# A hybrid transformer block: weight sums, spills, reloads and output DMAs moved between queues and in order

## The chip, the cores and the metric

One core of a Trainium2 chip runs the whole kernel. Its engines are PE (TensorE, matrix products), DVE (VectorE), ACT (ScalarE), POOL (GpSimd) and SP (SyncE, which here only issues DMAs). Each engine works through its own instructions in order. The metric is the device time of one execution in microseconds (us); the kernel before has a median of 2313.04 us in 3 runs (2312.16 to 2316.35).

## The reference

512 latent tokens and 256 context tokens of width 1024 go through two layers with shared weights. In short:

```
for l in range(2):
    sh1, sc1, g1, sh2, sc2, g2 = split(silu(c) @ w_ada[l] + b_ada[l])      # 6 modulation vectors, latents
    (the same for the context tokens, from c_ctx)
    h = rms_norm(x) * norm1_g * (1 + sc1) + sh1
    glu, q, k, v, rq, rk, rv, rg, gates = split(h @ w_in[l] + b_in[l])
    a   = silu(layer_norm(dwconv31(glu_a * sigmoid(glu_b))))                # convolution branch
    att = softmax attention: 8 query heads, 2 key/value heads, rotary, context keys for all
    ret = retention in both directions, chunks of 128, decay per head, group norm * silu(rg)
    y   = (ga * (a @ w_pa) + gb * (att @ w_pb) + gc * (ret @ w_pc)) @ w_out[l]
    x   = x + g1 * y
    h   = rms_norm(x) * norm2_g * (1 + sc2) + sh2
    gt, val = split(h @ w_up[l])                                            # 2 x 2816 columns
    x   = x + g2 * ((silu(dwconv3(gt)) * val) @ w_down[l])
out = rms_norm(x) * final_norm_g                                            # latents only
```

The context tokens do the same with their own modulation; in the last layer they only give keys, values and retention states.

## The kernel before

Activations lie feature by feature on 128 partitions, tokens along the free axis: a tile `x` is 128 features x 768 tokens. Every product in fp32 is made of three PE products of rounded halves: `whi*hh`, `whi*hl` and `wlo*hh`, where `whi`/`wlo` are the rounded weight and its rest, `hh`/`hl` those of the activation.

**Weights.** SP loads raw tiles of 512 KB (`raw`, `issue`), ACT rounds each to `whi` (L218), DVE subtracts to `wlo` (L219). SP looks two tiles ahead (RAWB).

**Start.** `start` loads x and the columns of `w_ada` in the pieces of START; `first_products` writes out the order of the first norm, of the modulation pieces (`go(stage, column)`) and of the first two column groups of `w_in` by hand, under `in_order`.

**Mixers.** `layer_mixers` goes through the units of ORDER: K, Q keys and queries, R retention inputs, A and C convolution, G gates, P the projection of the branches and T the third gate. Attention, retention, convolution and modulation are generators beside them (`Side`): each PE unit feeds them credit (`tick`), scaled by ATTR, RETR, CONVR and ADAR, and they emit their instructions in between. A scheduler then fixes the order on each engine. Four attention outputs `att` of 128 x 768 are spilled to DRAM (`attsp`, L1497) and reloaded as `rl` (L1503) for `w_pb`; all such tiles share 45 slots, so a new tile may wait until an older one's last reader, a spill too, is done. `ij` (L1583) is a table for retention; `ret_tables` makes `kdec` (L916) and `dec` (L930) from it.

**Sums.** In layer 0 the up-projection of the FFN is done with seven products of blocks in place of eight. Four of them need sums of weight blocks, S1 to S4. `make_sums` has POOL make them in DRAM: a copying DMA (L627) and adding DMAs (L632), six batches of up to four chunks, one batch at each of six units (SUMAT). The first DMA of a batch waits for the PE product before it in program order; S2 needs S1, S4 needs S2.

**Up-projection.** `up_order` lists the products: "11" and "12" for the first UPFIRST chunks, which need only one half of the tokens, then S2, S1, S3 for them, then the rest chunk by chunk. `last_chunks` runs `w_out` before it and steps the norm of the finished half of tokens; `split_tokens` makes the operands `hh`/`hl` (L716, L717) of the blocks.

**Modulation rows.** `ada_rows` makes late modulation vectors on DVE: POOL loads a row tile `rowa` into a raw slot (L588), DVE multiplies by `crow` and adds up (L599). During the down-projection `down` feeds it with ADAR[3]. The last down-projection's `evac` (L1814) adds to x.

**Output.** The final norm multiplies each x tile by `rstd` (L1550) and SP writes it (L1551), 16 DMAs.

Of the kernel before, what the change touches and what calls it, by code (L numbers as in the profile page):

```python
# [18 lines left out]
F32 = mybir.dt.float32  # L19
F32R = mybir.dt.float32r  # L20
AF = mybir.ActivationFunctionType
ALU = mybir.AluOpType
# [16 lines left out]
NSUB = 140  # L39
START = ((0, 256, 2), (256, 256, 0), (512, 256, 4), (768, 256, 0))  # L40
ND = 4
# [7 lines left out]
ATT_LEAD, RET_LEAD = (3, 2), (1, 1)  # L49
ATTR, RETR, CONVR, ADAR = (1.0, 1.0), (1.4, 1.6), (0.4, 0.4), (0.06, 0.28, 0.4, 0.33)  # L50
SUMAT = ("R1", "G1", "G2", "G3", "P1", "P2")
QLAG = 2
# [6 lines left out]
PEP, DVP, LATE = (4,), (2, 3), (5,)  # L59
NADA = 24 + 8 * len(PEP)  # L60
ROWS = 1552
# [35 lines left out]

UPFIRST = 3
CUTS = ((0, 4), (4, 8), (8, 12), (12, 16), (16, NFF))
# [185 lines left out]
class Kern:  # L285
# [92 lines left out]

    def last_chunks(self, key, xs, segs, hold, evac, norm, lead=0, limit=None):
# [14 lines left out]
        ws, tiles = [], []  # L394
        for m in range(KC - hold, KC):
            ws.append([])
            for k in range(n):
                ws[-1].append(self.W.next(key(m, k), P))
                if k == 0:
                    tiles.append(self.W.cur)  # L400
        tiles.append(self.W.cur + (self.W.off == SUB))
        gen = None
        halves = parts(segs)[::-1] if limit else parts(segs)
        for i, hs in enumerate(halves):
            for j, m in enumerate(range(KC - hold, KC)):
# [12 lines left out]
        self.W.release()  # L418
        return gen
# [200 lines left out]

    def make_sums(self, b):

        n = len(batches()[b]) * Q
        src = {x: self.io[f"wup{4 * b + i}"] for i, x in enumerate(BLOCKS)}
        for name, base, more in SUMS:
            t = src[name] = self.up_sums[b][name] = self.dram.tile([P, n], F32, name=f"sum{name}_{b}")
            first = self.nc.gpsimd.dma_start(t, src[base], max_dma_last_dim=2048)  # L627

            info = mybir.DependencyInfo(mybir.DependencyClass.Sync, mybir.DependencyReason.DATA)
            self.tc.add_manual_dep(first.ins, self.last_mm.ins.name, info, reason="later")  # L630
            for x in more:
                self.nc.gpsimd.dma_start(t, src[x], accum_op=ALU.add, max_dma_last_dim=2048)  # L632


    def rstd2(self, pts, name, y=None):
# [501 lines left out]
    def first_products(self, xs, ada):  # L1137
# [9 lines left out]

        def products(k, units=(0, 1)):
            for u in units:
                wh, wl = wb[u][k % 4]  # L1150
                for t in range(n):
                    pt = banks[u][t // 2][:, 256 * (t % 2):256 * (t % 2) + 256]
# [3 lines left out]

        def weights(c):
            self.W.limit = 2 * c + 2
            return [[self.W.next(("w_in", 0, k * P, col), 256) for k in range(4 * c, 4 * c + 4)] for col in (1536, 1024)]

# [5 lines left out]

        for k in range(KC):
            self.sq_add(k, xs[k], ALL, k == KC - 1)
        r = self.S("rstd")
        self.sq_rstd(ALL, r)  # L1170
        go(0, 0)
        go(1, 0)
        go(2, 0)
        banks = [[self.dps() if ND > 3 * u + v else self.ps() for v in range(n // 2)] for u in range(2)]
        t0 = m1(0)
        wb = weights(0)
        m2(t0, 0)
        t1 = m1(1)
        go(0, 256)
        go(1, 256)  # L1180
        m2(t1, 1)
        products(0)
        go(2, 256)
        t2 = m1(2)
        products(1)
        t3 = m1(3)
# [9 lines left out]
        m2(t4, 4)  # L1196
        wb = weights(1)
        go(0, 768)
# [340 lines left out]
    def out_norm(self, xs):  # L1539
# [4 lines left out]
        def gen(segs):  # L1544
# [4 lines left out]
            for k in range(KC):  # L1549
                nc.vector.tensor_tensor(xs[k][:, s], xs[k][:, s], r[:, s], op=ALU.mult)  # L1550
                nc.sync.dma_start(self.io["out"][k][:, s], xs[k][:, s])  # L1551
                yield
        return gen

    def layer_mixers(self, l, last, segs, T, xs, xsp, first, h2):
# [16 lines left out]
        def mixers():  # L1572
# [20 lines left out]
        ths, merged = [], [None] * KC  # L1593
        for step in ORDER[l].split():
            kind, i = step[0], int(step[1:] or 0)
# [49 lines left out]
        def evac(m, pts):  # L1645
            for pt, o, c in kinds(pts):
# [6 lines left out]
        return self.last_chunks(lambda m, k: ("w_out", l, k * P, m * P), mm, even(segs), HOLDO[l], evac, norm, LEADO,  # L1653
                                None if l else NUP + UPFIRST)

    def ffn(self, l, h2, xs, segs, T, gen, xsp, xup):
# [57 lines left out]
        def up_seven():  # L1714
# [37 lines left out]
            def s1(c):  # L1752
                Z[c] = (self.ps() if 0 < c < UPFIRST else self.dps())[:, :HALF]
                product(Z[c], "S1", c)
# [29 lines left out]
            for n, x in enumerate(up_order()):  # L1784
# [8 lines left out]
                elif x[0] != "S2" or x[1] >= UPFIRST:  # L1793
                    steps[x[0]](x[1])
                if n == 0:
                    next(gen)
# [194 lines left out]
```

## Time and profile before

| | us |
|---|---|
| median of 3 runs | 2313.04 |
| profiled execution, its own time | 2318.38 |
| its span | 2316.6 |
| PE busy | 2232.2 (96%) |
| DVE busy | 1604.8 (69%) |
| ACT busy | 989.0 (43%) |
| POOL busy | 144.5 (6%) |

The profile is of one execution. Busy is the time in which an engine works; issuing a DMA counts little. PE and DVE work most, at a mean granted clock of PE of 0.988 of full speed. PE's idle time is the difference between its busy time and the span; where it lies is shown in the rows below. Times there are from the start of the span. In a row `x2` is the number of instructions that it groups, and the square brackets give how long the engine stood idle before it and what released it.

### The profile page before, as it was taken

The numbers are of one execution on the slowest core, as the hardware profiler recorded it, in microseconds if no ns is written. First come the engines' busy times: TensorE is split into PE (matmuls) and PEld (weight loads), VectorE is DVE, ScalarE is ACT, GpSimd is POOL, SyncE is SP. The second block draws the span as 40 slices with busy tenths as digits, with TensorE's granted clock in tenths as the row PEclk, the third lists the DMA queues.
The fourth block names the chain that finished last, engine by engine and source line by source line (L and its number), as shares of the span: only waits on it lengthen the run. The fifth ranks groups of instructions, "written<-read, shape, count | busy, mean of one in ns | idle before, by whom it ended". The sixth has DMA issues, their size and how long they took to land.

```text
span 2316.6 us, 34409 instructions
## 1 busy us (share of the span) xinstructions
PE 2232.2 (96%) x13386; PEld 2037.1 (88%) x13386; DVE 1604.8 (69%) x3219; ACT 989.0 (43%) x1707; POOL 144.5 (6%) x225
## 2 busy tenths in 40 slices
PE   6999968999999989999999989999999999999998
PEld 5988958999999989999999979888887889888887
DVE  6876936889985567565655669878699756744445
ACT  3465643342242346554454434565343434423233
POOL 0001111100010000101101100000001100000000
PEclk9999989999999999999999999999999999999999
DMA  8226894813343333737647521111126623432221
GB/s 304 101 99 173 232 243 126 216 64 117 129 156 128 106 103 100 182 119 191 153 152 183 184 109 56 58 55 58 55 80 222 252 84 111 159 113 97 100 91 37
DMA packets 104466, 307.03 MB, mean 133 GB/s; under 512 B 11024, under 2 KB 13344, under 8 KB 104304
## 3 DMA queue, kind: packets, MB, share of 16 engines
q1 hardware_dynamic: 66240, 186.34, 23.5%
q0 software_dynamic: 38064, 118.50, 18.9%
q8 instruction: 105, 1.72, 0.3%
q14 instruction: 57, 0.47, 0.1%
HBM read 282.26 MB, written 68.68 MB: 151 GB/s over the span
## 4 chain that ended last, share of the span: by engine, by line
PE 53%; issue 3%; DVE 3%; DMA 1%; ACT 1%; POOL 0%; DVEq 0%; POOLq 0%; ACTq 0%
PE pd L319 31%; PE pd L1724 11%; PE ps L319 8%; PE ps L1724 2%; PE ps L1378 1%; DVE wlo L219 1%; DMA crow<-crow 0%; DMA rowa<-wadt 0%; ACT whi L218 0%; DVE cacc L827 0%; DMA rl<-attsp 0%; DVE qq L1326 0%; ACT dx L1805 0%; DMA raw<-wstream 0%; DVE rowa L599 0%
## 5 line engine op out<-in xcount | busy, mean ns | idle before, releaser
L218 ACT ACTIVATE whi<-raw 128x1024 fp32r<-128x1024 f32 x313 | 331.4, 1061 | 748.0 <-PE pd L319 492.0
L219 DVE TENSOR_TENSOR wlo<-raw,whi 128x1024 fp32r<-128x1024 f32 x313 | 382.3, 1222 | 258.8 <-ACT whi L218 245.1
L319 PE MATMUL pd<-hh,whi 128*128 128x384 f32 (+2 forms) x1472 | 471.1, 360 | 0.0
L319 PE MATMUL pd<-hh,wlo 128*128 128x384 f32 (+2 forms) x1472 | 470.2, 359 | 0.0
L319 PE MATMUL pd<-hl,whi 128*128 128x384 f32 (+2 forms) x1472 | 469.5, 359 | 0.0
L319 PEld LDWEIGHTS pd<-hh,whi 128*128 128x128 f32 x1472 | 270.9, 188 | 28.0 <-issue 1.8
L319 PEld LDWEIGHTS pd<-hh,wlo 128*128 128x128 f32 x1472 | 271.4, 188 | 25.9 <-issue 1.1
L319 PEld LDWEIGHTS pd<-hl,whi 128*128 128x128 f32 x1472 | 271.2, 188 | 25.9 <-issue 0.7
L827 DVE SCALAR_TENSOR_TENSOR cacc<-u,vec,cacc 128x497 f32<-128x497 f32 (+9 forms) x360 | 220.9, 650 | 2.0
L1724 PE MATMUL pd<-hh,whi 128*128 128x384 f32 x512 | 171.8, 339 | 9.1 <-ACT hh L716 9.1
L1724 PE MATMUL pd<-hl,whi 128*128 128x384 f32 x512 | 172.3, 336 | 0.5 <-DVE hl L717 0.4
L1724 PE MATMUL pd<-hh,wlo 128*128 128x384 f32 x512 | 171.7, 336 | 0.0
L1361 ACT ACTIVATE prob<-ps,amx,qrs 128x256 f32<-128x256 f32 (+1 forms) x144 | 93.8, 656 | 91.3 <-DVE amx L1356 74.9
L319 PE MATMUL pd<-whi,hl 128*128 128x256 f32 x416 | 120.3, 290 | 5.9 <-DVE hl L784 5.9
L319 PE MATMUL pd<-whi,hh 128*128 128x256 f32 x416 | 120.3, 292 | 2.1 <-ACT hh L781 2.1
L319 PE MATMUL pd<-wlo,hh 128*128 128x256 f32 x416 | 119.3, 287 | 0.0
L319 PE MATMUL pd<-hidh,whi 128*128 128x512 f32 (+1 forms) x302 | 104.1, 356 | 4.0 <-DVE x L1814 4.0
L1724 PEld LDWEIGHTS pd<-hh,whi 128*128 128x128 f32 x512 | 96.5, 189 | 12.0 <-ACT hh L716 10.1
L319 PE MATMUL pd<-hidl,whi 128*128 128x512 f32 (+1 forms) x302 | 103.1, 353 | 0.0
L319 PE MATMUL pd<-hidh,wlo 128*128 128x512 f32 (+1 forms) x302 | 102.9, 354 | 0.0
L599 DVE SCALAR_TENSOR_TENSOR rowa<-rowa,crow 128x768 f32<-128x768 f32 (+1 forms) x144 | 94.4, 686 | 8.9 <-DMA rowa<-wadt 8.9
L588 POOL DMA_DIRECT2D rowa<-wadt x72 | 39.1, 543 | 950.1 <-DVE wlo L219 737.1
(298 smaller groups left out, 4312.1 us busy)
## 6 DMA issues: line engine op xcount, KB each, us to landing
raw<-wstream SPq DMA_DIRECT2D x236, 512.0 KB, 3.5
rowa<-wadt POOLq DMA_DIRECT2D x72, 512.0 KB, 4.3
sumS<-wup POOLq DMA_DIRECT2D x30, 1024.0 KB, 13.0
raw<-sumS SPq DMA_DIRECT2D x88, 256.0 KB, 3.7
raw<-wup SPq DMA_DIRECT2D x66, 256.0 KB, 3.6
xup<-dx POOLq DMA_DIRECT2D x32, 384.0 KB, 7.2
sumS<-sumS POOLq DMA_DIRECT2D x10, 1024.0 KB, 9.7
adar<-wada SPq DMA_DIRECT2D x16, 384.0 KB, 7.6
```

What stands on the lines that cost most here:

```text
L218: nc.scalar.activation(hi, r, AF.Copy)
L219: nc.vector.tensor_tensor(lo, r, hi.bitcast(F32), op=ALU.subtract)
L319: self.last_mm = self.nc.tensor.matmul(out, w, x, start=start, stop=stop)
L588: nc.gpsimd.dma_start(loaded[-1], self.io["wadt"][l, 8 * pc + c])
L599: nc.vector.scalar_tensor_tensor(out, raw[:, a:b], 1.0, t[:, o:o + b - a], op0=ALU.mult, op1=ALU.mult, accum_out=acc[:, c, j, h:h + 1])
L827: nc.vector.scalar_tensor_tensor(acc[:, a:b], u[:, a + d:b + d], w(k), acc[:, a:b], op0=ALU.mult, op1=ALU.add)
L1361: nc.scalar.activation(pr[:, o - k0:o - k0 + c], pt[:, :c], AF.Exp, scale=rs, bias=mx[:, 2:3], accum_out=sm[:, j:j + 1])
L1378: nc.tensor.transpose(pt[:, b * P:b * P + P], pr[:, o + b * P:o + b * P + P], self.ident)
L1724: nc.tensor.matmul(pt, w[:, b], x, start=start and k == 0 and i == 0, stop=k == 3 and i == 2, skip_group_check=not start)
```

## The change

The changed kernel does seven things.
1. `spill` issues on ACT (`nc.scalar`) and `reload` and the load of `ij` on SP (`nc.sync`); all were on POOL.
2. `make_sums(n)` is called at every unit from the ninth on (SUMFROM). Step n makes the copies of batch n, S1 and S3 of batch n-1, S2 of n-2 and S4 of n-3, and each DMA waits for the PE product before it.
3. START has two pieces of 128 columns at first; `first_products` does the 512 latents first, with a norm of their own, then the 256 context tokens, and takes the weights of the two column groups one at a time.
4. UPFIRST is 4, and `up_order` does all "11" first and then all "12"; PACE sets how many steps of the norm follow each of the last four chunks of `w_out`, 3, 3, 1, 1, where there were 3 each. S1 of the first chunk takes its bank from the other pool.
5. ADAR[3] goes from 0.33 to 0.39.
6. The 16 output DMAs are issued by SP and ACT in turns.
7. NADA, slots for loaded modulation columns, goes from 24 to 26 (plus 8).

```diff
-START = ((0, 256, 2), (256, 256, 0), (512, 256, 4), (768, 256, 0))
+START = ((0, 128, 2), (128, 128, 0), (256, 256, 4), (512, 256, 0), (768, 256, 0))
-ATTR, RETR, CONVR, ADAR = (1.0, 1.0), (1.4, 1.6), (0.4, 0.4), (0.06, 0.28, 0.4, 0.33)
-SUMAT = ("R1", "G1", "G2", "G3", "P1", "P2")
+ATTR, RETR, CONVR, ADAR = (1.0, 1.0), (1.4, 1.6), (0.4, 0.4), (0.06, 0.28, 0.4, 0.39)
+SUMFROM = 8
-UPFIRST = 3
+PACE = (3, 3, 1, 1)
+UPFIRST = 4
-    out = [(n, c) for c in first for n in ("11", "12")] + [(n, c) for n in ("S2", "S1", "S3") for c in first]
+    out = [(n, c) for n in ("11", "12", "S2", "S1", "S3") for c in first]
...
-                    for _ in range(1 + KC // hold):
+                    for _ in range(pace[j] if pace else 1 + KC // hold):
...
-    def make_sums(self, b):
...
+    def make_sums(self, n):
+        steps = ((), ("S1", "S3"), ("S2",), ("S4",))
+        for b in range(len(batches())):
+            if not 0 <= n - b < len(steps):
+                continue
...
+            for name, base, more in SUMS:
+                if n == b:
+                    t = sums[name] = self.dram.tile([P, len(batches()[b]) * Q], F32, name=f"sum{name}_{b}")
+                    ops.append(nc.gpsimd.dma_start(t, src[base], max_dma_last_dim=2048))
+                elif name in steps[n - b]:
+                    for x in more:
+                        ops.append(nc.gpsimd.dma_start(sums[name], src[x] if x in src else sums[x], accum_op=ALU.add,
+                                                       max_dma_last_dim=2048))
+            for op in ops:
+                self.tc.add_manual_dep(op.ins, self.last_mm.ins.name, info, reason="later")
...
+        t0 = self.modulated1(0, xs[0], r, 0, 0, lat)
+        wb = [weights(0, 0)]
+        self.modulated2(0, t0, 0, 0, lat, h0)
+        self.h.append(h0)
+        wb.append(weights(0, 1))
+        products(0, (0,), th)
+        self.rstd2([(y[1], *ctx[0])], "rstd", r)
+        t0 = self.modulated1(0, xs[0], r, 0, 0, ctx)
+        self.modulated2(0, t0, 0, 0, ctx, h0)
+        go(0, 128)
+        products(0, (1,), th)
+        go(1, 128)
+        products(0, (0,), tc)
+        go(2, 128)
+        t1 = m1(1)
+        products(0, (1,), tc)
+        m2(t1, 1)
...
-        self.nc.gpsimd.dma_start(dst[:, :w], t[:, :w])
+        self.nc.scalar.dma_start(dst[:, :w], t[:, :w])
...
-            self.nc.gpsimd.dma_start(t[:, :w], src[i][:, :w])
+            self.nc.sync.dma_start(t[:, :w], src[i][:, :w])
...
-                nc.sync.dma_start(self.io["out"][k][:, s], xs[k][:, s])
+                (nc.sync, nc.scalar)[k % 2].dma_start(self.io["out"][k][:, s], xs[k][:, s])
...
-            nc.gpsimd.dma_start(self.ij[:, :4 * P + 2], io["ij"])
+            nc.sync.dma_start(self.ij[:, :4 * P + 2], io["ij"])
...
-            if l == 0 and step in SUMAT:
-                self.make_sums(SUMAT.index(step))
+            if l == 0 and n >= SUMFROM:
+                self.make_sums(n - SUMFROM)
```

Lines of the changed kernel stand 1 to 32 further down. Its order on the engines differs as follows.

POOL in layer 0 before, around the third spill and `ij`; `sumS_2` is the third batch of sums, `attsp_104` the third spill.
```order
L627 DMA sumS_3_3439<-wup 512x512
L632 DMA sumS_3_3436<-wup 512x512
L632 DMA sumS_3_3439<-sumS_3_3433 512x512
L627 DMA sumS_3_3442<-wup 512x512
L1497 DMA attsp_104<-att_3067 128x768
L632 DMA sumS_3_3442<-sumS_3_3439 512x512
L1583 DMA ij_3988<-ij 128x514
L1497 DMA attsp_105<-att_3712 128x768
```
In the changed kernel POOL has sums alone there; this is ACT around the same spill, `att` being the tile that is spilled and `whi` a weight.
```order
L1411 ACTIVATE probt_3589<-ps_3596 128x256
L1425 ACTIVATE att_3099<-ps_3600 128x128
L1529 DMA attsp_104<-att_3099 128x768
L1393 ACTIVATE prob_3618,asm_3614<-ps_3607,amx_3613,qrs_878 128x512
L1393 ACTIVATE prob_3618,asm_3614<-ps_3608,amx_3613,qrs_878 128x256
L1411 ACTIVATE probt_3624<-ps_3625 128x512
```
The spill moved from among the sums to the place right behind the last write of its `att`.

SP in the changed kernel, layer 1, around the reloads `rl`; the raw tiles are weights.
```order
L200 DMA raw_17143<-wstream 128x1024
L200 DMA raw_17216<-wstream 128x1024
L1535 DMA rl_17187<-attsp_102 128x512
L1535 DMA rl_17189<-attsp_103 128x512
L1535 DMA rl_17191<-attsp_104 128x512
L1535 DMA rl_17193<-attsp_105 128x512
L200 DMA raw_17262<-wstream 128x1024
```
Before, the same four stood on POOL between row loads:
```order
L588 DMA rowa_2_6_17135<-wadt 128x1024
L588 DMA rowa_2_7_17201<-wadt 128x1024
L1503 DMA rl_17139<-attsp_102 128x512
L1503 DMA rl_17141<-attsp_103 128x512
L1503 DMA rl_17143<-attsp_104 128x512
L1503 DMA rl_17145<-attsp_105 128x512
L588 DMA rowa_3_0_17205<-wadt 128x1024
```
The reloads left the queue of the row loads for that of the weights.

DVE before, between the last chunk of the FFN (`hidl`) and the first x of the last down-projection in layer 0, where eight products of modulation rows (L599) stand; these are the last two of them and what follows.
```order
L599 SCALAR_TENSOR_TENSOR rowa_0_7_12603,adag_11014<-rowa_0_7_12603,crow_9184 128x768
L599 SCALAR_TENSOR_TENSOR rowa_0_7_12603,adag_11014<-rowa_0_7_12603,crow_9185 128x256
L219 TENSOR_TENSOR wlo_12767<-raw_12563,whi_12766 128x1024
L604 TENSOR_TENSOR mod_88<-adag_11014 128x16
L605 TENSOR_TENSOR mod_88<-mod_88,vec_87 128x16
L1814 SCALAR_TENSOR_TENSOR x_12619<-pd_12690,mod_85,x_12619 128x512
```
And in the changed kernel, at the same place:
```order
L1807 SCALAR_TENSOR_TENSOR fy_12655<-fg_12498,vec_83,fy_12655 128x255
L1811 TENSOR_TENSOR fv_12499<-fv_12499,fy_12655 128x768
L450 TENSOR_TENSOR hidl_12664<-fv_12499,hidh_12663 128x768
L1846 SCALAR_TENSOR_TENSOR x_12667<-pd_12738,mod_85,x_12667 128x512
L220 TENSOR_TENSOR wlo_12815<-raw_12627,whi_12814 128x1024
L1846 SCALAR_TENSOR_TENSOR x_12667<-pd_12739,mod_85,x_12667 128x256
```
The row products are gone from there.

## Rows read from the trace of the kernel before

**Rows 1.** Stretches: us, busy us (rows) by engine, PEclk, DMA, GB/s
```profile
240.00:280.00 40.00, 40.00 (x302) 36.67 (x299) 38.76 (x98) 25.40 (x67) 6.95 (x8) 1.00 0.91 215
340.00:360.00 20.00, 8.21 (x51) 7.85 (x52) 0.00 (x0) 1.66 (x6) 2.20 (x3) 0.63 0.95 220
```

**Rows 2.** Timeline of PE around 351: start, us, work [idle <- releaser]
```profile
351.79 1.98 PE L319 MATMUL ps<-probt,vt 128*64 128x128 f32 x16 [23.90 <-ACT probt L1379]
...
364.90 1.59 PE L319 MATMUL ps<-rq,rk 64*128 64x128 f32 x8 [3.45 <-DVE kb L981]
```

**Rows 3.** Waits of PE, one line: us in total, times, longest
```profile
PE pd L1724 <- ACT hh L716: 9.1, 3, 6.7
```

**Rows 4.** Timeline of PE around 1337
```profile
1337.14 0.78 PE L319 MATMUL pd<-hidh,whi 128*128 128x512 f32 x2 [3.99 <-DVE x L1814]
...
1341.40 0.51 PE L319 MATMUL pd<-hidl,whi 128*128 128x512 f32 x2
```

**Rows 5.** Timeline of PE around 1768
```profile
1768.12 0.79 PE L319 MATMUL pd<-brh,whi 128*128 128x512 f32 x1 [4.41 <-ACT brh L448]
```

**Rows 6.** Timeline of ACT from 295 to 366
```profile
296.02 0.30 ACT L1393 ACTIVATE att<-ps 128x128 f32<-128x128 f32 x1
...
315.18 0.57 ACT L1361 ACTIVATE prob<-ps,amx,qrs 128x256 f32<-128x256 f32 x1 [0.86 <-DVE amx L1358]
...
351.35 0.38 ACT L1379 ACTIVATE probt<-ps 128x256 f32<-128x256 f32 x1 [24.87 <-DMA attsp<-att]
...
361.00 0.49 ACT L916 ACTIVATE kdec<-lg,ij 128x8 f32<-128x8 f32 x2 [6.91 <-DMA ij<-ij]
```

**Rows 7.** Timeline of POOL from 330 to 352
```profile
334.25 1.04 POOL L632 DMA_DIRECT2D sumS<-wup  x1 [14.76 <-DMA sumS<-wup]
...
337.75 0.96 POOL L1497 DMA_DIRECT2D attsp<-att  x1
```

**Rows 8.** The tile attsp, spills and reloads together: last line of its view
```profile
DMA to landing us min/median/max: 2.3/4.5/13.5
```

**Rows 9.** DMA issues, 232 to 327: count, KB, median us to landing
```profile
raw<-wstream SPq DMA_DIRECT2D x7, 512.0 KB, 7.3
attsp<-att POOLq DMA_DIRECT2D x1, 384.0 KB, 13.2
```

**Rows 10.** Timeline of SP's DMA queue from 290 to 366
```profile
291.55 29.05 SPq L199 DMA_DIRECT2D raw<-wstream  x3
```

**Rows 11.** The tile ij: last line of its view
```profile
DMA to landing us min/median/max: 3.2/6.3/9.5
```

**Rows 12.** Timeline of POOL around 504
```profile
504.83 0.58 POOL L588 DMA_DIRECT2D rowa<-wadt  x1 [47.86 <-DVE wlo L219]
```

**Rows 13.** Timeline of PE in the first up-projection products
```profile
848.29 0.33 PE L1724 MATMUL pd<-hh,whi 128*128 128x384 f32 x1
...
862.17 0.34 PE L1724 MATMUL ps<-hh,wlo 128*128 128x384 f32 x1
```

**Rows 14.** Timeline of DVE around 1332
```profile
1330.01 0.95 DVE L599 SCALAR_TENSOR_TENSOR junk<-rowa,crow 128x768 f32<-128x768 f32 x1
...
1334.56 0.42 DVE L599 SCALAR_TENSOR_TENSOR rowa<-rowa,crow 128x256 f32<-128x256 f32 x1
```

**Rows 15.** Timeline of POOL around 1763
```profile
1762.79 0.53 POOL L588 DMA_DIRECT2D rowa<-wadt  x1 [5.66 <-DVE rowa L599]
1763.31 2.13 POOL L1503 DMA_DIRECT2D rl<-attsp  x4
```

**Rows 16.** The tile rl: last line of its view
```profile
DMA to landing us min/median/max: 4.1/4.5/6.4
```

**Rows 17.** Timeline of PE at the start
```profile
29.59 0.38 PE L319 MATMUL pd<-whi,hl 128*128 128x256 f32 x1 [2.13 <-DVE hl L784]
```

**Rows 18.** Timeline of DVE at the end
```profile
2309.73 2.77 DVE L1550 TENSOR_TENSOR x<-x,rstd 128x256 f32<-128x256 f32 x8
```

**Rows 19.** Timeline of SP's DMA queue at the end
```profile
2301.67 12.33 SPq L1551 DMA_DIRECT2D out_t<-x  x16
```

More of the change, by code (lines that the diff above doesn't have):

```diff
@@ L59 @@
 PEP, DVP, LATE = (4,), (2, 3), (5,)
-NADA = 24 + 8 * len(PEP)
+NADA = 26 + 8 * len(PEP)
 ROWS = 1552
@@ L377, in dense, with last_chunks @@
         return pts
-    def last_chunks(self, key, xs, segs, hold, evac, norm, lead=0, limit=None):
+    def last_chunks(self, key, xs, segs, hold, evac, norm, lead=0, limit=None, pace=None):
         n = len(xs)
@@ L619, in up_operand @@
         return t[:, j * Q:j * Q + Q]
-    def make_sums(self, b):
[L623 to L632, printed above, removed]
+    def make_sums(self, n):
+        nc = self.nc
+        info = mybir.DependencyInfo(mybir.DependencyClass.Sync, mybir.DependencyReason.DATA)
+        steps = ((), ("S1", "S3"), ("S2",), ("S4",))
+        for b in range(len(batches())):
+            if not 0 <= n - b < len(steps):
+                continue
+            sums = self.up_sums[b]
+            src = {x: self.io[f"wup{4 * b + i}"] for i, x in enumerate(BLOCKS)}
+            ops = []
+            for name, base, more in SUMS:
[8 more added lines that the diff above has]
+                self.tc.add_manual_dep(op.ins, self.last_mm.ins.name, info, reason="later")
     def rstd2(self, pts, name, y=None):
@@ L1146, in go, with products @@
                     next(part)
-        def products(k, units=(0, 1)):
+        def products(k, units=(0, 1), ts=range(n)):
             for u in units:
                 wh, wl = wb[u][k % 4]
-                for t in range(n):
+                for t in ts:
                     pt = banks[u][t // 2][:, 256 * (t % 2):256 * (t % 2) + 256]
@@ L1155, in products, with weights @@
                         self.mm(pt, x, y, k == 0 and i == 0 and t % 2 == 0, k == KC - 1 and i == 2 and t % 2 == 1)
-        def weights(c):
-            self.W.limit = 2 * c + 2
-            return [[self.W.next(("w_in", 0, k * P, col), 256) for k in range(4 * c, 4 * c + 4)] for col in (1536, 1024)]
+        def weights(c, u):
+            self.W.limit = 2 * c + u + 1
+            return [self.W.next(("w_in", 0, k * P, (1536, 1024)[u]), 256) for k in range(4 * c, 4 * c + 4)]
         m1 = lambda k: self.modulated1(0, xs[k], r, 0, k, ALL)
@@ L1165, in m2 @@
             self.modulated2(0, t, 0, k, ALL, self.h[k])
[L1167 to L1171, printed above, removed]
+        for k in range(KC - 1):
+            self.sq_add(k, xs[k], ALL)
+        for seg in ALL:
+            self.sq_add(KC - 1, xs[KC - 1], [seg])
+        r, y = self.S("rstd"), []
+        lat, ctx = ([seg] for seg in ALL)
+        th, tc = range(SEQ // P), range(SEQ // P, n)
+        h0 = (self.S("hh", F32R), self.S("hl", F32R))
+        for (o, c), in (lat, ctx):
+            y.append(self.ps()[:, :c])
+            self.mm(y[-1], self.ones, self.sq[:, o:o + c], True, True)
+            if o == 0:
+                go(0, 0)
         go(1, 0)
+        self.rstd2([(y[0], *lat[0])], "rstd", r)
         go(2, 0)
         banks = [[self.dps() if ND > 3 * u + v else self.ps() for v in range(n // 2)] for u in range(2)]
-        t0 = m1(0)
-        wb = weights(0)
-        m2(t0, 0)
+        t0 = self.modulated1(0, xs[0], r, 0, 0, lat)
[12 more added lines that the diff above has]
+        go(2, 128)
         t1 = m1(1)
+        products(0, (1,), tc)
+        m2(t1, 1)
         go(0, 256)
         go(1, 256)
-        m2(t1, 1)
-        products(0)
+        products(1, (0,))
         go(2, 256)
         t2 = m1(2)
-        products(1)
+        products(1, (1,))
         t3 = m1(3)
@@ L1196, in first_products @@
         m2(t4, 4)
-        wb = weights(1)
+        wb = [weights(1, u) for u in range(2)]
         go(0, 768)
@@ L1593, in layer_mixers @@
         ths, merged = [], [None] * KC
-        for step in ORDER[l].split():
+        for n, step in enumerate(ORDER[l].split()):
             kind, i = step[0], int(step[1:] or 0)
@@ L1653, in layer_mixers @@
         return self.last_chunks(lambda m, k: ("w_out", l, k * P, m * P), mm, even(segs), HOLDO[l], evac, norm, LEADO,
-                                None if l else NUP + UPFIRST)
+                                None if l else NUP + UPFIRST, None if l else PACE)
     def ffn(self, l, h2, xs, segs, T, gen, xsp, xup):
@@ L1752, in s1 @@
             def s1(c):
-                Z[c] = (self.ps() if 0 < c < UPFIRST else self.dps())[:, :HALF]
+                Z[c] = (self.ps() if c < UPFIRST else self.dps())[:, :HALF]
                 product(Z[c], "S1", c)
@@ L1794, in up_seven @@
                     steps[x[0]](x[1])
-                if n == 0:
+                if n == 1:
                     next(gen)
```

## Prediction

> **What bounds the kernel now.** I read the table of stretches first. Where nothing goes wrong TensorE (PE) is busy all of a stretch: 40.00 of 40 us from 240 to 280 [rows 1], although the DMA engines are 91% busy there. So a gain is what PE stands idle for a reason that the change removes, and nothing that another engine saves. Then I looked for the stretches that fall short. From 340 to 360 PE works 8.21 of 20 us at a mean granted clock of 0.63, and VectorE (DVE) does nothing, so no work piles up that would claim the time later [rows 1]. The timeline of PE gives the places of the gaps in square brackets: 23.90 us up to 351.79 and 3.45 up to 364.90 [rows 2], 3.99 up to 1337.14 [rows 4], 4.41 up to 1768.12 [rows 5]; the list of waits gives 9.1 us in three pieces for hh, line 716, the longest 6.7 [rows 3]. Together 44.85 us.
>
> Each gap is then followed back. The big one waits for ScalarE's (ACT) probt at 351.35, which itself stood 24.87 us for the DMA attsp<-att [rows 6]: the new tile takes the slot of a written att, and may not before that is spilled. Att's last write is at 296.02 [rows 6], but POOL issues its spill at 337.75 only, after a weight sum that waited 14.76 us at 334.25 [rows 7]. So a small transfer stood 41 us in POOL's in-order queue behind sums that wait for each other. The 3.45 us go back the same way: kdec waits 6.91 us for ij [rows 6], also issued by POOL behind a sum.
>
> After such gaps the clock is low: the matmul pairs from 1337.14 last 0.84 us each, those from 1341.40 0.51 [rows 4]. Seven pairs start in the 4.26 us between. At full clock a product of 384 columns takes 0.187 (76 of them in 14.22 us [rows 13]), so a pair of 512 and 256 takes 0.374 and seven pairs 2.6. A gap thus costs about 1.6 us behind it.
>
> **The change part by part.**
> Spills. ACT issues them, right behind the last write of att. Issue near 296.3 instead of 337.75; the slot is wanted at 315.18 at the earliest [rows 6], 18.9 us later. The longest landing of a spill or a reload of it is 13.5 [rows 8], the spill issued between 232 and 327 took 13.2 [rows 9]. It fits with 5 us to spare, so 23.90 goes. An issue by ACT is in no row; POOL's own take 0.96 [rows 7]. Four in a layer between 0 and 0.96 us are hidden, as ACT is not waited for by PE there.
>
> ij. SP issues it behind a raw tile whose issue ends at 320.60 [rows 10]. Landing takes 3.2 to 9.5 [rows 11], so it is there at 324 to 331, say 322 + 9.5 = 331.5. Kdec would have run at 361.00 - 6.91 = 354.1, which is 330.2 once the 23.9 are gone: late by 1.3 at most. Of 3.45 I count 2.8. With two low-clock stretches (2 x 1.5, a little under the 1.6 above, since what stays of the 3.45 may leave some of it) the hole is worth 23.9 + 2.8 + 3.0 = 29.7.
>
> The sums are moved from six units to units 8 to 16 of the list, one step each. They are as many bytes. Before they begin at R1; now at G1, three units later, and the last waits for the second unit T. Before, the sums had 24 us of DMA time while PE was idle; now all lie beside PE. That costs nothing if raw tiles still come in time: under sums they land in 7.3 us [rows 9] and PE stayed full [rows 1]. Bounds 0 and 7.3 us (one tile late by its whole landing); I take 2, nearer to the row of the full stretch.
>
> The Trainium skill bears on the spill (page "DMA: Bandwidth & Descriptors", section "Issuing engines are not separate DMA queues"): DMAs started by any engine run on the same 16 DMA engines, and starting them elsewhere saves only the issuing time. By that rule the spill gains no more than its 0.96 us of issue of the 25.4 counted for it (23.9 and 1.5), and the total would be near 2292; but the row shows 41 us spent before the issue, in waiting, which the rule does not count, so I follow the row. What remains of the rule is the danger to landing, which is the first rival.
>
> Up-projection. PE ran six block products of 12 matmuls and four ones-products of the norm from 848.29 to 862.51, then waited to 869.16 for S2's hh [rows 3, 13]. Now eight stand before S2, 24 x 0.187 = 4.5 us more, up to 867.0. The chain to that hh is DVE and ACT work; the norm begins a little sooner by PACE, and gets one more evacuation and weight split in its way. I take 868.5, a gap of 1.5 instead of 6.7. The two later gaps (the other 2.4 of 9.1) are covered by the fourth chunk of S2 and S1. Saved: 9.1 - 1.5 = 7.6, minus 0.8 for later small waits; nothing for the clock, which may fall all the same. Bounds 3 (hh some 4 us later) and 10.7 (no gap, and the clock's 1.6 with it).
>
> Modulation rows. Before x, line 1814, DVE still did rows from 1330.01 to 1334.98 [rows 14], and PE's pd banks came free only at 1337.14. At the higher rate they lie inside the last down-projection. PE stopped at 1333.15 (1337.14 - 3.99), and its order ends the product that the first x reads six matmuls, about a microsecond, before that; x is two pieces like the 0.42 of a row's 256 columns [rows 14], 0.8. So the gap shrinks from 3.99 to about 0.3: 3.7 + 1.6 for the clock = 5.3. Bounds 0 (the stall moves to the x<-xup reload on POOL) and 5.6.
>
> Reloads of layer 1. POOL issues rl at 1763.31 behind a row load at 1762.79 that waited 5.66 [rows 15]. On SP they go between raw tiles, at about 1758; landing 4.1 to 6.4 [rows 16] brings the first at 1762 to 1764.5, brh 0.6 later; before, PE stopped at 1763.71 (1768.12 - 4.41). So 4.41 shrinks to 0 to 1.5: with the clock I count 5.0, bounds 0 and 6.0. Reloads of layer 0 were not waited for.
>
> Start. PE waits 2.13 us up to 29.59 for hl [rows 17]. Latents first brings hl forward by about that; but the second product now needs a further 128-column piece of the modulation. Bounds -2.1 and +2.1 (the wait once more, or gone); I take 0, since DVE decides the stage and its work is the same.
>
> Output. DVE ends its last products at 2309.73 + 2.77 = 2312.50 [rows 18], SP's issues end at 2301.67 + 12.33 = 2314.00 [rows 19]. Two queues can save 1.0 of the 1.5; bounds 0 and 1.5. On this the Trainium skill says (page "Perfetto Trace Analysis", section "DMA Instruction — HWDGE (DVE, Sync)") that such issues lock one shared descriptor generator; by that it is 0. No run here shows ACT issuing. I take 0.7.
>
> Sum: 29.7 - 2 + 6.8 + 5.3 + 5.0 + 0 + 0.7 = 45.5. The profiled execution took 2318.38 us (span 2316.6), 5.3 over the median; 2318.4 - 45.5 = 2272.9, and against the median 2313.0 - 45.5 = 2267.5. As small new waits are commoner than small new gains I forecast 2269.
>
> **The rivals.**
> *The spill lands later.* The sums now run steadily while all four spills go out, and if a landing of 13.2 grows past 18.9, PE waits again, us for us. At 25 us two of the spills cost 6 each and the clock 2 x 1.6: about 2284. For it: a DMA share of 0.91 and more around them [rows 1]. Against: 13.2 was measured at that share.
> *The sums end late.* Crow and the row loads stand behind the sums on POOL. Before, POOL had been idle 47.86 us when it issued the first row load at 504.83 [rows 12], so the sums may end 48 us later than they did. They begin three units later, but before they also stood still between batches. Should they end late: rows crowd into DVE, which brings the 1337 gap back, 5.3, and costs as much again: 2280.
> *Slower: SP blocked.* Raw tiles are issued in order by SP. If a reload or ij waits there for a slot that is freed only by work fed from the next raw tiles, PE starves, as long as the wait lasts. Four rl tiles need four slots at once; with a wait of some 45 us at either reload the whole gain is eaten: 2313 or above. Against: on POOL they went out four in 2.13 us, without a wait between them [rows 15], and the slots' earlier users are ahead of them.
> *It does not do what it says.* The order might keep the spill late on ACT; the rows of the new order put it directly behind att, so I give it next to nothing.
>
> **How the numbers follow.** Forecast 0.66 (its own range 2261 to 2279), spill 0.12, sums 0.10, SP blocked 0.06, something unknown to the extent of half the gain (2290) 0.06. The range 2260 to 2290 leaves out the blocked SP and tails. Within 0.2% (4.6 us) is what a measurement cannot tell from no change. Faster 0.92, same 0.03, slower 0.05.
>
> **What would show it.** Right: no gap above 3 us between 325 and 370; attsp issues by ACT within 1 us of att; PE's wait for hh, line 716's successor, under 4 us; none at the first x of the last down-projection above 1; raw landings unchanged near 1760. Wrong: a wait of PE on probt with attsp as its releaser; a raw issue on SP that stands over 20 us behind rl or ij; DVE rows still ahead of x. The forecast as a whole fails if the waits go and others of the same size stand in the stretch 370 to 480, where the sums now lie.

## The result and the profile after

The changed kernel takes 2278.24 us (median of 4 runs, 2276.52 to 2280.47) beside 2313.11 us of the kernel before (median of 4 runs here, 3 above; 2312.16 to 2316.35): a ratio of 0.9847, 95% interval 0.983 to 0.9864. Forecast were 2269 us, with 2260 to 2290 as the range. So the time lies in the range and the direction is right; the gain is 34.9 us where 44 were forecast. In the profile the span goes from 2316.6 to 2276.4 us, the mean granted clock from 0.988 to 0.996.

Where the 40.2 us of the span went is read from the two traces by taking the same product of PE in each, and the time from one such place to the next:

| stretch of PE, from the place before | before | changed | difference | forecast |
|---|---|---|---|---|
| start to the first attention product (ps<-kh,qq) | 124.70 | 127.19 | +2.5 | 0 |
| to the first product of a branch (pd<-brh) | 384.82 | 353.29 | -31.5 | -27.7 (hole -29.7, sums +2) |
| to the first product of the up-projection | 338.77 | 338.71 | -0.1 | 0 |
| to its last product | 473.36 | 473.61 | +0.3 | -6.8 |
| to the first query product of layer 1 (ps<-cst,qdd) | 87.97 | 82.21 | -5.8 | -5.3 |
| to layer 1's first branch product | 315.85 | 315.78 | -0.1 | 0 |
| to the first product of w_out in layer 1 | 171.14 | 166.95 | -4.2 | -5.0 |
| to PE's last product | 411.20 | 411.20 | 0 | 0 |
| to the end of the span | 8.79 | 7.46 | -1.3 | -0.7 |

The hole is gone. The stretches that answer to [rows 1], of the changed kernel:
```profile
320.00:340.00 20.00, 19.81 (x176) 17.77 (x175) 10.47 (x26) 11.67 (x33) 6.70 (x8) 1.00 0.76 176
340.00:360.00 20.00, 20.00 (x137) 18.84 (x136) 16.53 (x34) 5.21 (x8) 0.00 (x0) 1.00 1.10 265
```
PE is full at a DMA share of 1.10. ACT's timeline in the same place answers to [rows 6]:
```profile
297.42 0.33 ACTq L1529 DMA_DIRECT2D attsp<-att  x1
...
330.75 0.49 ACT L927 ACTIVATE kdec<-lg,ij 128x8 f32<-128x8 f32 x2 [0.40 <-ACT att L1425]
```
The spill is issued at once, and kdec waits for att, no more for ij. How fast things land while the sums run, from 232 to 327 (name, engine, count, KB, median us), beside [rows 9]:
```profile
sumS<-wup POOLq DMA_DIRECT2D x16, 1024.0 KB, 20.2
raw<-wstream SPq DMA_DIRECT2D x7, 512.0 KB, 6.8
...
attsp<-att ACTq DMA_DIRECT2D x2, 384.0 KB, 4.9
ij<-ij SPq DMA_DIRECT2D x1, 257.0 KB, 3.7
```
The raw tiles come as before (6.8 against 7.3) and PE is full, so no cost of the sums to PE shows, where I had put 2 us. The two spills land in 4.9 us in the median, where the one of [rows 9] took 13.2.

In the up-projection the first wait falls as forecast, from 6.7 to 1.70, but others come. PE's timeline, beside [rows 3, 13]:
```profile
839.00 0.97 PE L1756 MATMUL pd<-hh,whi 128*128 128x384 f32 x4 [1.70 <-ACT hh L727]
...
869.52 0.97 PE L1756 MATMUL pd<-hh,whi 128*128 128x384 f32 x4 [2.08 <-ACT hh L727]
...
915.54 0.44 PE L1756 MATMUL pd<-hh,whi 128*128 128x384 f32 x1 [1.10 <-ACT whi L219]
...
918.19 0.44 PE L1756 MATMUL pd<-hh,wlo 128*128 128x384 f32 x1 [2.03 <-DVE wlo L220]
```
Idle time in the whole stage goes only from 10.27 to 8.34 us (sum of PE's gaps between the two places of the table), and the rest, PE's own products, takes 465.3 instead of 463.1, as the clock falls after three gaps in place of one: the mean granted clock is 0.91 from 839 to 859, from 869 to 889 and from 915 to 935 and 1.00 between; before it is 0.88 from 862 to 890 and 1.00 on both sides.

The last down-projection, the modulation rows gone. DVE's timeline, beside [rows 14]:
```profile
1300.27 0.96 DVE L450 TENSOR_TENSOR hidl<-fv,hidh 128x768 fp32r<-128x768 f32 x1 [0.91 <-ACT hidh L449]
1303.15 0.75 DVE L1846 SCALAR_TENSOR_TENSOR x<-pd,mod,x 128x512 f32<-128x512 f32 x1 [1.92 <-PE pd L320]
```
Now DVE waits for PE, and PE has no gap there. The reload in layer 1, beside [rows 5], and the start, beside [rows 17], in PE's timeline:
```profile
1730.01 0.50 PE L320 MATMUL pd<-brh,whi 128*128 128x512 f32 x1 [0.94 <-ACT brh L449]
```
```profile
17.09 1.94 PE L320 MATMUL ps<-adar,cc 128*32 128x128 f32 x32
...
24.99 0.58 PE L320 MATMUL pd<-whi,hh 128*128 128x256 f32 x1 [4.15 <-ACT hh L792]
...
28.61 1.94 PE L320 MATMUL ps<-adar,cc 128*32 128x128 f32 x32
...
34.43 2.00 PE L320 MATMUL ps<-adar,cc 128*32 128x256 f32 x32
```
The first product comes 2.1 us sooner (24.99; 27.07 before), but a piece of 128 columns needs as many modulation products, 32 in 1.94 us, as one of 256, and there is one piece more. The end, DVE and SP, beside [rows 18, 19]:
```profile
2270.86 2.77 DVE L1582 TENSOR_TENSOR x<-x,rstd 128x256 f32<-128x256 f32 x8
```
```profile
2262.80 10.85 SPq L1583 DMA_DIRECT2D out_t<-x  x8
```
DVE ends at 2273.63, SP's last issue at 2273.65, where it had trailed by 1.5.

### The profile page after: what moved, and what is told of

Same layout as the page of the kernel before. It is cut to its first block, busy times and chain, and to the rows that moved or that the text cites. A ratio compares the mean times of both kernels' runs of the same rounds, so it can differ in the third digit from the quotient of the medians.

```text
span 2276.4 us, 34457 instructions
## 1 busy us (share of the span) xinstructions
PE 2228.6 (98%) x13418; PEld 2036.9 (89%) x13418; DVE 1607.1 (71%) x3235; ACT 988.2 (43%) x1708; POOL 133.9 (6%) x207
## 4 chain that ended last, share of the span: by engine, by line
PE 85%; issue 6%; DVE 5%; DMA 2%; ACT 1%; POOL 0%; SPq 0%; DVEq 0%; POOLq 0%; ACTq 0%
PE pd L320 58%; PE ps L320 13%; PE pd L1756 9%; PE ps L1756 2%; PE ps L1410 2%; DVE wlo L220 1%; DMA adar<-wada 1%; DMA raw<-wstream 1%; ACT whi L219 1%; DVE cacc L838 1%; PE ps L1323 0%; DMA xup<-dx 0%; DMA rowa<-wadt 0%; DVE ht L783 0%; DVE qq L1358 0%
## 5 line engine op out<-in xcount | busy, mean ns | idle before, releaser
L1756 PE MATMUL pd<-hh,whi 128*128 128x384 f32 x496 | 166.8, 340 | 5.3 <-ACT hh L727 4.1
```

The lines of the kernel that those rows point to most:

```text
L1756: nc.tensor.matmul(pt, w[:, b], x, start=start and k == 0 and i == 0, stop=k == 3 and i == 2, skip_group_check=not start)
```

## The experiments

Twelve runs were made in three lots of four; two of them repeat a kernel. The kernel before ran beside each lot: medians 2315.68, 2318.65 and 2315.85 us, single runs from 2309.3 to 2323.0. So a difference of 3 us between lots says little, and ratios to the kernel before are given.

**Which move closed the hole?** Five kernels. First the spills alone, in the kernel before:
```diff
-        self.nc.gpsimd.dma_start(dst[:, :w], t[:, :w])
+        self.nc.scalar.dma_start(dst[:, :w], t[:, :w])
```


> The kernel before with the four spills of a layer issued by ACT, nothing else. Theory (both waits come from one queue, and the load of ij stands behind the same sums): ij is still issued by POOL near 350, kdec runs near 361 whatever the spill does, and TensorE's wait for probt is replaced by a wait for kb of 24 to 28 us that ends near 365; time 2309 to 2313. Rival (the two waits add up as in the prediction's sum): the 23.9 us go, the 3.45 us stay; time 2286 to 2289.

Measured: 2316.08 us, ratio 1.0007 (0.9996 to 1.0019), no gain at all. PE's and POOL's timelines:
```profile
358.13 1.59 PE L319 MATMUL ps<-rq,rk 64*128 64x128 f32 x8 [24.79 <-DVE kb L981]
```
```profile
345.42 1.00 POOL L632 DMA_DIRECT2D sumS<-sumS  x1 [13.79 <-DMA sumS<-wup]
346.05 0.97 POOL L1583 DMA_DIRECT2D ij<-ij  x1
```
The theory holds. PE no longer waits 23.9 us for probt, it waits 24.79 us for kb (retention keys scaled by kdec), which needs ij, which POOL issues behind the same sums as ever. The two waits [rows 2] ended within 14 us of one another, one after the other behind the same queue; the 3.45 us of the second were only what the first had left of it.

All three moved (spills on ACT; reloads and ij on SP), the rest as before:
```diff
-            self.nc.gpsimd.dma_start(t[:, :w], src[i][:, :w])
+            self.nc.sync.dma_start(t[:, :w], src[i][:, :w])
...
-            nc.gpsimd.dma_start(self.ij[:, :4 * P + 2], io["ij"])
+            nc.sync.dma_start(self.ij[:, :4 * P + 2], io["ij"])
```


> The kernel before with spills on ACT, reloads and ij on SP; sums, start, up-projection, modulation rate and output as before. Theory (queues alone close the hole): no gap over 1 us between 325 and 370, the hole's 30 us and the layer 1 reload's 4 us gone; time 2276 to 2281. Rival (the new schedule of sums is needed as well): a gap of 5 us or more stays there or between 370 and 480; time above 2285.

Measured: 2283.56 us, ratio 0.9861 (0.9845 to 0.9878). No gap between 325 and 370; from the first attention product to the first branch product 353.30 us, as good as in the changed kernel (353.29). The time is 2.6 us over the range that I expected, since the reload left 2.16 us of gap; but the hole is closed with the old sums, so their new schedule has no part in it. The kernel before with ij alone on SP was not run: that the 23.90 us for the spill would stay there is likely by [rows 2, 6], but not shown.

The opposite: the changed kernel with those three put back on POOL (the same lines the other way).


> The changed kernel with spills, reloads and ij put back on POOL; the new schedule of sums and all else as changed. Theory (what matters is the queue): the spill of the third att is issued near 298, but lands 13 to 30 us later because it stands in POOL's own DMA queue behind 1 MB copies; ij is issued after the fourth spill, near 331, and lands as late; a gap of 5 to 25 us in 315 to 365 and 4 us at the layer 1 reload; time 2288 to 2305. Rival (sums that no longer wait on one another are enough): no gap over 1 us there, only the 4 us of the reload; time 2281 to 2284.

Measured: 2313.55 us, ratio 0.9985 (0.9973 to 0.9997). Nearly the whole gain is lost: PE stands 25.7 us up to 372.24. That is 8 us over the range of the theory and far from the rival, so the new schedule alone does nothing for the hole either. To see which of the three mattered there, ij alone was put back on POOL:


> The changed kernel with the load of ij alone put back on POOL. Theory (a small load in POOL's DMA queue lands behind the 1 MB copies in it): ij is issued near 335, lands some 20 us later, and a gap of 20 to 26 us returns before 365; 2298 to 2306. Rival (in the run with everything on POOL the fourth spill ahead of ij was what made it late): ij is there by 345, a gap under 12 us; 2286 to 2292.

Measured: 2307.65 us, ratio 0.9966 (0.9957 to 0.9976). POOL's, ACT's and PE's timelines:
```profile
328.21 2.10 POOL L641 DMA_DIRECT2D sumS<-sumS  x2 [35.38 <-PE ps L320]
329.50 2.88 POOL L641 DMA_DIRECT2D sumS<-wup  x2
330.75 4.16 POOL L638 DMA_DIRECT2D sumS<-wup  x4
338.96 0.56 POOL L1615 DMA_DIRECT2D ij<-ij  x1 [4.05 <-issue]
```
```profile
369.69 0.49 ACT L927 ACTIVATE kdec<-lg,ij 128x8 f32<-128x8 f32 x2 [23.59 <-DMA ij<-ij]
```
```profile
372.45 1.15 PE L320 MATMUL pd<-hh,whi 128*128 128x384 f32 x2 [27.09 <-ACT rk L1468]
```
It is issued at 338.96 and lands 30.7 us later, at 369.67, where SP's took 3.7. Seven of the eight sums above it, 1 MB each, were still on their way when it was issued; the last of them landed at 369.06. ACT is ready for kdec at 346.1 (369.69 - 23.59), so a landing within 7 us would have held up nothing. ACT waits for it with kdec, and behind kdec, in order, stands the evacuation of rk (retention keys) that PE needs.

In the profiles of all kernels the table's stretch up to the first branch product goes by the queue of ij: it takes 353.2 to 353.8 us in the ten with ij on SP and 380.6 to 384.8 in the four with ij on POOL. And the spills alone on POOL:


> The changed kernel with the spills alone put back on POOL. Theory (with the new schedule of sums a spill is issued at once, its long landing of up to 30 us hits no slot that is wanted sooner): no gap over 1 us between 300 and 370, within 2 us of the changed kernel. Rival (the prediction's slack of 18.9 us after the last write of att counts): TensorE waits for probt some 10 us; 2288 or more.

Measured: 2278.61 us, ratio 0.9847 (0.9829 to 0.9864), the time of the changed kernel, without a gap in the place, although a spill took up to 32.1 us to land. The last line of the tile attsp's view, and the DMA issues from 254 to 255 and from 297 to 298, the second and the third spill:
```profile
DMA to landing us min/median/max: 2.2/5.3/32.1
```
```profile
attsp<-att POOLq DMA_DIRECT2D x1, 384.0 KB, 2.6
```
```profile
attsp<-att POOLq DMA_DIRECT2D x1, 384.0 KB, 26.5
```
The second spill finds no sum on its way (the copies issued before it had landed by 250.2) and lands in 2.6 us from POOL, too. The third and the fourth have sums ahead of them in the queue and land 1.0 and 0.2 us after the last of these. So what delays a small transfer is its place behind the sums. The third spill is the one to which I gave 18.9 us from [rows 6]; its slot was not wanted for at least 26.5, so those 18.9 us were no limit.

**The start.** The changed kernel with the old start, twice, the second time beside the spill run above:
```diff
-START = ((0, 128, 2), (128, 128, 0), (256, 256, 4), (512, 256, 0), (768, 256, 0))
+START = ((0, 256, 2), (256, 256, 0), (512, 256, 4), (768, 256, 0))
...
-        t0 = self.modulated1(0, xs[0], r, 0, 0, lat)
+        t0 = m1(0)
...
```
NADA goes back to 24 with it, here and in every run below that has pieces of 256 columns; it was not tried apart.

> The changed kernel with the old start: pieces of 256 columns, latents and context together. Theory (the new start costs 2.5 us at 125 us, of which 1.4 are given back by 245 since DVE decides between): 1 us faster than the changed kernel, 2277 to 2277.5. Rival A: the whole 2.5 come out at the end, 2275.7. Rival B (the new start was a gain that the comparison of places hides): slower, 2279 or more.

> The changed kernel with the old start, once more, on the chip of the other three. Theory: 2272 to 2276, ratio to before 0.981 to 0.983. Rival (its first time was an easy chip): 2277 or more.

Measured: 2273.08 us, ratio 0.9821 (0.9805 to 0.9837), and 2275.92, 0.9828 (0.9812 to 0.9844). The changed kernel as a control, in the second lot, beside neither of these two:


> The changed kernel once more, as the control beside the other three. Theory: its ratio to the kernel before is 0.9847 again (0.983 to 0.9865), and its places lie within 1 us of those of its first profile. Rival (the 5 us by which the kernel with the old start was ahead lay in the chip): the ratio is 0.982 or 0.983.

Measured: 2277.58, ratio 0.9826 (0.9808 to 0.9845), which is nearer to the rival than to the theory. Ratios therefore don't tell the two starts apart; the absolute medians do, weakly: 2277.58 to 2278.61 in three runs with the new start (one with its spills on POOL), 2273.08 and 2275.92 with the old one. The traces say more. From the first norm product to the first attention product eight profiles with the old start take 108.4 to 111.2 us (mean 109.6), five with the new one 110.9 to 112.1 (mean 111.5): some 2 us lost, though the two ranges touch. What loses them was tried by keeping latents first, with 256 columns and no fifth piece:
```diff
-        go(0, 128)
+        t1 = m1(1)
         products(0, (1,), th)
-        go(1, 128)
+        go(0, 256)
+        m2(t1, 1)
         products(0, (0,), tc)
-        go(2, 128)
-        t1 = m1(1)
+        go(1, 256)
         products(0, (1,), tc)
...
```


> The changed kernel with the latents first as in its new start, but pieces of 256 columns as in the old one, so that there is no fifth round of modulation. Theory (what the new start lost was the fifth round, and latents first gains the 2 us by which the first product is earlier): 4 to 7 us faster than the changed kernel, level with the kernel with the old start or up to 2 us ahead of it. Rival (the loss is in splitting latents and context): 1 to 4 us slower than the kernel with the old start.

Measured: 2275.35 us, ratio 0.9829 (0.9813 to 0.9845); the stretch takes 109.6. So it is level with the old start in the same lot, and 3 us ahead of the spill run, which has the new start: as far as one profile and these 3 us tell, the fifth piece was the loss, and latents first by itself is worth nothing that can be measured.

**Up-projection, modulation rate and output**, all on the kernel with the old start. First UPFIRST, the order and the pace as before:
```diff
-UPFIRST = 4
+UPFIRST = 3
...
-    out = [(n, c) for n in ("11", "12", "S2", "S1", "S3") for c in first]
+    out = [(n, c) for c in first for n in ("11", "12")] + [(n, c) for n in ("S2", "S1", "S3") for c in first]
...
-                                None if l else NUP + UPFIRST, None if l else PACE)
+                                None if l else NUP + UPFIRST, None)
...
```
The bank of the first S1 and the place of one step of the operands' making go back with them.

> The changed kernel with the old start and the old up-projection: three first chunks in the old order, three steps of the norm after each chunk. Theory (what the fourth chunk covers at S2 is given back at later waits and low clock): within 2 us of the kernel with the old start alone, ratio to before 0.981 to 0.983; from the first to the last up-projection product 473 to 474.5 us. Rival (the term of the prediction, 6.8 us, is there but hidden by something else in the comparison): 5 to 8 us slower, ratio 0.9845 to 0.9855.

Measured: 2279.99 us, ratio 0.9838 (0.9819 to 0.9856), 4 to 7 us over the kernel with the old start; in its profile, of an execution 3.3 us over the median, the stage takes 478.1 us, where it takes 471.7 to 475.0 in the eight profiles with four chunks, their order as changed and the higher rate (0.39). My theory fell here, and the rival came nearer: undone in the changed kernel, the part is worth about 5 us. But the three profiles with three chunks and the old rate (0.33) have 473.4 to 474.6. What differs is the modulation rate: with the old order and 0.39, PE waits once more for ACT in the first down-projection and the clock falls there (0.89 granted in the 15 us that follow).
```profile
928.71 0.69 PE L320 MATMUL ps<-hidh,whi 128*128 128x384 f32 x1 [2.40 <-ACT dx L1816]
```
Idle is 11.84 us in the stage, against 9.53 to 10.27 with three chunks and the old rate. Then rate and output undone together, in places that the trace keeps apart:
```diff
-ATTR, RETR, CONVR, ADAR = (1.0, 1.0), (1.4, 1.6), (0.4, 0.4), (0.06, 0.28, 0.4, 0.39)
+ATTR, RETR, CONVR, ADAR = (1.0, 1.0), (1.4, 1.6), (0.4, 0.4), (0.06, 0.28, 0.4, 0.33)
...
-                (nc.sync, nc.scalar)[k % 2].dma_start(self.io["out"][k][:, s], xs[k][:, s])
+                nc.sync.dma_start(self.io["out"][k][:, s], xs[k][:, s])
```


> The changed kernel with the old start, ADAR[3] at 0.33 as before and all output DMAs on SP. Theory: the wait of 4 us for the first x of the last down-projection is back, and with the low clock behind it 5.5 to 6 us are lost there; 1 to 1.5 us more at the end; 6.5 to 7.5 us over the kernel with the old start. Rival (with the spills gone from POOL the row loads come earlier and the rows are done in time at 0.33): nothing lost there, 1 to 1.5 us in all.

Measured: 2282.09 us, ratio 0.9845 (0.9827 to 0.9864). The wait is back:
```profile
1306.01 1.01 PE L320 MATMUL pd<-hidh,whi 128*128 128x512 f32 x2 [3.99 <-DVE x L1825]
```
From the last up product to layer 1's first query product it takes 89.2 us against 82.0, and from PE's end to the span's 8.9 against 7.5: 7.2 and 1.4 us. The second is as the theory said, the first more than its 5.5 to 6. By the other profiles the first is 5.7 to 6.1: the stretch takes 87.9 to 88.1 us in the three others with the old rate and 82.0 to 82.2 in all ten with the higher one. The end takes 8.8 to 9.1 in all four with SP alone and 7.4 to 7.9 in all ten with SP and ACT in turns. The up-projection takes 472.3, within the range that it has with the higher rate; so the higher rate costs nothing that shows beside four chunks, and 3.5 to 4.7 us beside three.

Last, an attempt to get rid of the new waits at 915 and 918: each down-projection after S3 of its chunk.
```diff
-        if c in CUTAT:
-            out.append((CUTAT[c],))
         out += [("12", c), ("S2", c), ("S1", c), ("S3", c)]
+        if c in CUTAT:
+            out.append((CUTAT[c],))
```


> The changed kernel with the old start, and each down-projection put after S3 of its chunk instead of before the chunk's 12. Theory (the new waits for whi and wlo after the first down-projection, 1.1 and 2.0 us with the clock behind them, come from weight splits that stand on ACT and DVE behind the work on the chunk just finished by S4): the two waits go, 3 to 5 us faster than the kernel with the old start, ratio 0.980. Rival (the splits wait for slots that TensorE frees, wherever the down-projection stands): the waits move or stay, within 1.5 us.

Measured: 2280.92 us, ratio 0.9843 (0.9822 to 0.9863): slower than either expected. The wait of 2.0 for wlo is gone; one of 0.97 for whi is left, now ahead of the down-projection. But the down-projections now wait for ACT to empty their banks, 7.3 us in seven places (the profile is of an execution 4.7 us over the median). PE's timeline shows two of them:
```profile
935.15 0.44 PE L320 MATMUL ps<-hidh,whi 128*128 128x384 f32 x1 [2.31 <-ACT dx L1816]
```
```profile
1224.02 1.31 PE L320 MATMUL ps<-hidh,whi 128*128 128x384 f32 x2 [2.69 <-ACT dx L1816]
```

## Why the prediction was right, and where not

**The hole** was sized right (31.5 against 29.7 and a cost of 2), its mechanism was right, and its split was wrong. "A small transfer stood 41 us in POOL's in-order queue behind sums": so it was, and all that had to go from POOL did. The prediction also asked, rightly, whether ij on SP would be in time (331.5 against 330.2; it landed at 326.59). But "so 23.90 goes" gives that time to the spills and 2.8 to ij, and as prices of single moves these fail: the spills alone are worth nothing in either kernel (1.0007 in the old, the time unchanged in the new), ij alone is worth about 29 us in the new one (2307.65 against 2278.24 and, with spills on POOL, 2278.61). The sum came out because ij was moved as well; what the spills' move adds under the old schedule of sums, with ij on SP, is not shown.

**Spills that land later**, the first rival, did not come true: they land sooner, in 2.3 to 9.2 us from ACT while the sums run under the new schedule; and under it even 26.5 us cost nothing.

**SP blocked**, the third, did not come true either: the four reloads of layer 1 go out in 1.97 us from 1723.18, and raw tiles land in 4.7 us around them, as before.

**The sums** cost nothing, neither beside PE (raw 6.8) nor by ending late: the last sum is issued at 474.19 and the first row load at 475.78, 29 us earlier than before (504.83 in [rows 12]), as is their first use by DVE, at 506.23 instead of 535.26.

**Up-projection** is the step that failed: 6.8 us forecast as saved, 0.3 lost. (The second profile of the changed kernel has 471.7 us in the stage, a gain of 1.7; none of the eight with this part and the higher rate comes near 466.6.) S2's wait fell to 1.70 as worked out (1.5). "The two later gaps are covered by the fourth chunk" was wrong: one became 2.08 (hh stands on ACT behind a weight split that waits for PE), and two of 1.10 and 2.03 for weight splits appeared at the first down-projection. The waits for hh still add up to 4.1 us. In the profile shown the clock falls behind each of these gaps; in the second profile of the same kernel it stays at 1.00 behind the waits of 1.70 and 2.08 and falls only at the down-projection. What the runs add is that the part is not lost: it pays for the higher modulation rate, which costs some 4 us with three chunks. From the first up product to layer 1 neither takes 561.3 to 562.6 us (three profiles), rate 0.39 with three chunks 560.1, four chunks with 0.33 561.5 (one profile each), both 553.9 to 557.2 (eight). The time of the run with three chunks and 0.39 says the same; why the rate brings PE the extra wait for ACT was not tried.

**Modulation rows** came out at 5.8 (5.3), the **reload** at 4.2 (5.0), the **output** at 1.3 (0.7). The reload's remainder isn't steady: PE waits from 0.1 to 3.83 us in the profiles with reloads on SP, and the stretch takes 165.8 to 170.8 us in them, against 170.5 to 171.1 with reloads on POOL. The longest is that of the kernel with the old start, the second time, where reloads took up to 10.3 to land:
```profile
1728.74 0.60 PE L320 MATMUL pd<-brh,whi 128*128 128x512 f32 x1 [3.83 <-ACT brh L449]
```

**The start** was put at 0 with bounds of 2.1 and lost 2.5 by the two traces, 2 by the means. "DVE decides the stage and its work is the same" was wrong: a fifth piece is a fifth round of products, transposes and coefficients, and its 32 products take as long at 128 columns as at 256 (1.94 and 2.00 us).

**The base.** The sum missed by 5.3 us (45.5 against 40.2 of span). Part of that is luck: up-projection, start and reload fell short by 10.4 together, and the hole, whose cost of 2 for the sums did not come, gave back 3.8. Another 5.3 came from taking the sum off the median, 2313.04, though it was worked out on an execution 5.3 us longer. In all lots the kernel before ran from 2309.3 to 2323.0: the profiled one was an ordinary one, and the median of three on the low side. Why its spread is wider than the changed kernel's (2275.2 to 2280.5) stays open: the hole alone does not make it, since the kernel with ij back on POOL has the hole and runs from 2306.6 to 2310.5.

The likeliest fastest of the kernels that ran is the changed one with the old start, or with latents first and 256 columns: 2273 to 2276 us against 2277.6 to 2278.6, a difference that the ratios do not confirm.

## What to carry to other kernels

A wait that ends last hides the next one behind the same queue: before a gap is priced, take its releaser away on paper and ask when the next consumer of that queue would be served. A small load that something waits for doesn't belong in the DMA queue in which bulk copies run, even if it is issued early. Two edits that load and relieve the same engines are to be timed together and apart; here, by the means of the stretch, four chunks alone were worth 0.6 us, the higher rate alone 2.0, and both together 6.5.

## What the runs showed of the hardware

The same 257 KB land in 30.7 us from POOL's queue behind seven sums of 1 MB, and in 2.9 to 3.7 from SP's beside the same sums (7.6 beside the old schedule). Spills behind such sums land in 26.5 to 32.1 from POOL's queue, in 2.6 when none is ahead of them, and in 9.2 at most from ACT's. The Trainium skill (page "DMA: Bandwidth & Descriptors", section "Issuing engines are not separate DMA queues") says that starting DMAs on other engines only saves the issuing time. Here it saved 27 us of landing, and the measurement decides. Another section of that page of the Trainium skill ("Queues, rings and completion order") has the DMA engines take turns between the queues packet by packet. With that the traces agree as far as landings show it: what stands in another queue than the sums does not wait for their landing.

An issue of a spill takes ACT 0.33 to 0.35 us and POOL 0.54 to 1.24; an output DMA takes ACT 0.34 to 0.38 and SP 0.33 to 0.41. ACT and SP in turns ended the output 1.3 to 1.4 us sooner, so whatever they share did not undo it. From the Trainium skill (page "Perfetto Trace Analysis", section "DMA Instruction — HWDGE (DVE, Sync)"), which has one generator locked by each issue, the prediction had worked out 0; the measurement decides here, too, and how long such a lock lasts no run shows.

After a gap of the same length the clock fell in some executions and not in others. From 50 to 70 us the kernel before and the second run with the old start have the same wait of 2.35 us:
```profile
50.00:70.00 20.00, 17.62 (x148) 16.16 (x148) 15.87 (x47) 9.08 (x14) 0.00 (x0) 0.91 0.48 152
```
```profile
50.00:70.00 20.00, 17.63 (x160) 16.17 (x160) 17.23 (x54) 8.97 (x14) 0.00 (x0) 1.00 0.46 152
```
At a granted clock of 0.91 PE gets through 148 matmuls, at 1.00 through 160. From the first norm product to the first attention product the two take 110.0 and 108.4 us, a difference almost as large as that of the edit there; how much of it the clock makes was not taken apart.
